# A fused two-layer matmul on one core: magnitude sums moved, a new start, and sums of w2 in another order

## The chip, the cores and the metric

The kernel runs on one core of one Trainium2 chip. The metric is the device time of one execution in microseconds (us). A run's time is its span in the profile plus about 1.55 us. All runs told here are of one core, and all were recorded as being in the fast one of the two states that a kernel's executions can show.

Engines are named as in the profile: PE multiplies, PEld loads its weights, DVE is VectorE, ACT is ScalarE, POOL is GpSimd, SP issues DMAs. A bank is the memory in which PE adds up products; in this kernel ACT or DVE reads it out before PE goes on in it.

## The reference

```python
y = np.matmul(x, w1) + b1      # x: 16 x 512 x 768 fp32, w1: 768 x 3072
y = np.maximum(y, 0)
return np.matmul(y, w2)        # w2: 3072 x 768, result fp32
```

## The kernel before

The rows of x (8192) are worked in blocks of 1024, and the 3072 hidden columns in two chunks. Each product is done by a Strassen-Winograd scheme: seven products in place of eight, with sums of the operands' quarters made by DVE. Block 0 multiplies x by w1 plainly (`first_plain`), since x and w1 come straight from the DMA then. ACT also makes magnitude sums of x, w1 and w2 (sums of squares, for w1 of fourth powers); only at the end are they looked at, to see whether fp16 was safe.

The parts that the change touches:

```python
def sums_w(self, w):                       # DVE, four sums of a weight tile
    for o, i, j in ((self.T3, self.B12, self.B22), (self.T1, self.B12, self.B11),
                    (self.T2, self.B22, self.T1), (self.T4, self.B21, self.T2)):
        self.nc.vector.tensor_tensor(out=w[:, o], in0=w[:, i], in1=w[:, j], op=ALU.subtract)
# T1 lies in the place of B12

def stat_w(self, stat, c, t, w):           # ACT, one magnitude sum
    ...
    if stat == "w1":
        self.nc.scalar.activation(out=junk, in_=src, func=ACTF.Square)
        src = junk
    self.nc.scalar.activation(out=junk, in_=src, func=ACTF.Square, accum_out=...)

# second(): one group of seven products of the second layer; bank "a" is used again and again
def p1(): mm(g["a"], self.A11, self.B11, True); copy("s1", g["a"], 0, 0)   # ACT copies
def p2(): ...                              # DVE adds to the output
def p6(): mm(g["a"], self.S2, self.T2, False); copy("s2", g["a"], 0, 1)    # needs p1's copy
...
def p7(): mm(g["a"], self.S3, self.T3, False); add(out(1, 1), g["a"], g["s5"])
def p4(): mm(g["a"], self.A22, self.T4, False); ...                        # needs p7's add

# run(): the start
self.transpose_x_first(0)                  # four row blocks of x, by PE, casts by DVE and ACT
self.turn_bias(rows)
# plan(): hooks that run after a named step, (group kind, block, group, step)
put("p1", 0, 1, 1, self.transpose_x_first, 1)      # the second 512 rows (xn), after t=1
...
```

The order of PE's work at the start is then: transposes of the first 512 rows, their products with w1 tiles 0 and 1, transposes of the second 512 rows (xn), their products with tiles 0 and 1, then tiles 2 to 5. A group's steps are interleaved with those of the next group, so between p1 and p6, and between p7 and p4, PE does three other steps.

## Time and profile before

| what | before |
|---|---|
| median of 4 runs | 907.83 us (906.83 to 907.95) |
| profiled run | 906.39 us, span 904.8 us |
| PE busy | 885.0 us, 98% of the span |
| PE's idle time that the waits name | 5.4 ACT, 5.2 first x, 1.4 sums of w2, 0.9 and 0.8 at the end |

The prediction shows the lines.

### The profile page before, as it was taken

What the parts mean: (1) busy time and instruction counts of PE and PEld (TensorE: products, weight loads), DVE (VectorE), ACT (ScalarE), POOL (GpSimd) and SP (SyncE); (2) the same over time, 40 slices, a digit from 0 to 9 for tenths busy, and PEclk for the clock granted to TensorE, in tenths of its full rate; (3) what the DMA queues carried; (4) which work ended last, traced back from release to release, by engine and by line L of the source; (5) the groups of instructions that cost most, each with busy time, mean ns of one, the idle gap of its engine ahead of it and who ended that gap; (6) DMA issues with size and microseconds to landing.
All of it is one profiled execution on the core that took longest, in us unless ns stands there. A gap on an engine that the chain in (4) does not pass through costs nothing. (4 is left out here: it accounts for less than half of the span.)

```text
span 904.8 us, 13016 instructions
## 1 busy us (share of the span) xinstructions
PE 885.0 (98%) x4775; PEld 468.7 (52%) x4775; DVE 551.9 (61%) x1013; ACT 425.0 (47%) x710; POOL 83.5 (9%) x143
## 2 busy tenths in 40 slices
PE   7999979999999999999999999999999999999997
PEld 4454444554545545455554545545455554545544
DVE  2597726557465565636737667576675757667564
ACT  4757696775555555534435048453513315042220
POOL 7200000000000100021101000100001010010100
PEclk9999999999999999999999999999999999999999
DMA  9999969678584964584849344644445354350613
GB/s 202 201 239 189 338 126 279 132 178 228 126 280 105 278 137 129 223 201 122 183 144 424 135 150 158 209 157 170 130 189 191 123 197 176 134 175 35 210 52 125
DMA packets 106471, 162.52 MB, mean 180 GB/s; under 512 B 67852, under 2 KB 81956, under 8 KB 104356
## 3 DMA queue, kind: packets, MB, share of 16 engines
q1 hardware_dynamic: 67696, 114.44, 36.6%
q0 software_dynamic: 38384, 46.41, 26.0%
q8 instruction: 39, 0.64, 0.3%
q10 hardware_dynamic: 324, 0.80, 0.2%
q14 instruction: 28, 0.23, 0.1%
HBM read 95.37 MB, written 76.48 MB: 190 GB/s over the span
## 5 line engine op out<-in xcount | busy, mean ns | idle before, releaser
L441 PEld LDWEIGHTS <-y 128*128 128x128 f16 x2688 | 263.4, 98 | 194.9 <-issue 10.2
L363 PEld LDWEIGHTS <-w1s 128*128 128x128 f16 x1890 | 185.0, 98 | 212.5 <-issue 1.7
L441 PE MATMUL a<-w2s,y 128*128 128x384 f16 x1536 | 277.5, 327 | 7.8 <-ACT s L454 5.4
L363 PE MATMUL a<-x,w1s 128*128 128x512 f16 x1080 | 267.8, 379 | 0.8 <-DVE y L373 0.8
L369 ACT ACTIVATE s<-a,b1y 128x512 f32<-128x512 f32 x180 | 123.7, 687 | 305.4 <-PE a L363 302.3
L363 PE MATMUL c<-x,w1s 128*128 128x512 f16 x540 | 145.9, 379 | 0.1
L441 PE MATMUL c<-w2s,y 128*128 128x384 f16 x768 | 145.7, 326 | 0.0
L319 DVE TENSOR_TENSOR y<-y 128x512 f16<-128x512 f16 x96 | 40.8, 425 | 116.1 <-ACT y L405 103.7
L446 DVE TENSOR_TENSOR o<-a,s 128x384 f32<-128x384 f32 x64 | 35.6, 556 | 83.4 <-PE a L441 73.3
L373 DVE CUSTOM_DVE_ANT_0 y<-a,s 128x512 f16<-128x512 f32 x90 | 61.7, 685 | 32.2 <-ACT s L369 32.0
L405 ACT ACTIVATE y<-a,b1y 128x512 f16<-128x512 f32 x90 | 61.8, 687 | 28.5 <-PE a L363 28.4
L441 PE MATMUL b<-w2s,y 128*128 128x384 f16 x384 | 73.2, 327 | 0.0
L363 PE MATMUL b<-x,w1s 128*128 128x512 f16 x270 | 73.0, 379 | 0.0
L426 POOL DMA_DIRECT2D o<-out_dram x64 | 34.1, 538 | 389.6 <-DMA out_dram<-o 225.6
L321 DVE TENSOR_TENSOR y<-y 128x1024 f16<-128x1024 f16 x96 | 66.4, 692 | 3.3
L369 ACT ACTIVATE s<-c,b1y 128x512 f32<-128x512 f32 x90 | 61.9, 688 | 8.1 <-PE c L363 8.1
L454 ACT ACTIVATE s<-a 128x384 f32<-128x384 f32 x64 | 31.3, 488 | 70.4 <-PE a L441 70.4
L373 DVE CUSTOM_DVE_ANT_0 y<-b,s 128x512 f16<-128x512 f32 x90 | 61.6, 684 | 3.0 <-PE b L363 1.3
L373 DVE CUSTOM_DVE_ANT_0 y<-c,s 128x512 f16<-128x512 f32 x90 | 61.5, 683 | 0.4
L446 DVE TENSOR_TENSOR o<-b,s 128x384 f32<-128x384 f32 x64 | 35.6, 556 | 26.3 <-PE b L441 15.6
L256 ACT ACTIVATE junk<-xn 128x768 f16<-128x768 f16 x60 | 50.5, 842 | 0.3
L446 DVE TENSOR_TENSOR s<-a,o 128x384 f32<-128x384 f32 x64 | 35.6, 556 | 19.5 <-PE a L441 19.5
(67 smaller groups left out, 421.7 us busy)
## 6 DMA issues: line engine op xcount, KB each, us to landing
out_dram<-o SPq DMA_DIRECT2D x127, 384.0 KB, 3.3
o<-out_dram POOLq DMA_DIRECT2D x64, 384.0 KB, 4.0
xd<-x SPq DMA_DIRECT2D x8, 2688.0 KB, 12.7
x<-xd SPq DMA_DIRECT2D x8, 2688.0 KB, 9.7
xn<-in_x_dram POOLq DMA_DIRECT2D x15, 768.0 KB, 10.6
w1s<-in_w_dram POOLq DMA_DIRECT2D x24, 192.0 KB, 6.6
w2d<-w2t SPq DMA_DIRECT2D x6, 672.0 KB, 4.4
w2s<-w2d SPq DMA_DIRECT2D x6, 672.0 KB, 9.3
```

What stands on the lines that cost most here:

```text
L256: self.nc.scalar.activation(out=junk[:, 0:2].rearrange("p a n -> p (a n)"), in_=rows, func=ACTF.Square, accum_out=self.stat[:, i:i + 1])
L319: tt(out=y[:, self.S1], in0=y[:, self.A21], in1=y[:, self.A22], op=ALU.add)
L321: tt(out=y[:, self.S3:self.S2 + 1:self.S2 - self.S3], in0=y[:, self.A21:self.S1 + 1], in1=a11, op=ALU.subtract)
L363: nc.tensor.matmul(ps, lhsT=w[:, slot, k, :], rhs=x[:, xslot, k, :], start=(start and k == 0), stop=(k == 2), skip_group_check=True)
L369: nc.scalar.activation(out=g[name], in_=ps, func=ACTF.Identity, bias=bias)
L373: nc.vector._custom_dve(TENSOR_ADD_SAT, out=y[:, slot], in0=ps, in1=g[s], s0=F_MAX, s1=0.0)
L405: nc.scalar.activation(out=y[:, self.A21], in_=g["a"], func=ACTF.Relu, bias=bias1)
L426: self.nc.gpsimd.dma_start(out=o[:, half, :], in_=self.rows_of(it, j, half))
L441: nc.tensor.matmul(ps, lhsT=ys[t][:, op, j * P:(j + 1) * P], rhs=ws[t][:, slot, :], start=(start and t == 0), stop=(t == self.TP - 1), ski ...
L446: nc.vector.tensor_tensor(out=o, in0=ps, in1=s, op=ALU.add)
L454: nc.scalar.activation(out=to, in_=ps, func=ACTF.Copy)
```

## The change

Three independent things. The magnitude sums of w1 and w2, which stood in blocks 1 and 2 two to a group, go one by one into the last groups of blocks 1 to 6 (those of the second chunk, in blocks 9 and 10 before, go one to a group into blocks 8 to 10). At the start PE works on a tile of ones until x comes, and the first rows are transposed and multiplied in two parts of 256 rows. And of the sums of w2, the two that are used first (T1, T2) are made first for all tiles, and T3, T4 after; T3 instead of T1 now lies in the place of B12. The sums of w1 use the same function, so they too are made in the new order, T1, T2, T3, T4.

```diff
+        every = ((self.T1, self.B12, self.B11), (self.T2, self.B22, self.T1),
+                 (self.T3, self.B12, self.B22), (self.T4, self.B21, self.T2))
...
-        self.transpose_x_first(0)
-        self.turn_bias(rows)
+        self.warm()                                  # nine products of ones
+        self.transpose_x_first(0, (0, 1))
+        self.hooks["p1", 0, 0, 0] = [lambda: self.transpose_x_first(0, (2, 3)),
+                                     lambda: self.turn_bias(rows)]
...
-            put("p1", 0, *at, lambda t: self.sums_w(self.w2s[t]), t)
+            put("p1", 0, *at, lambda t: self.sums_w(self.w2s[t], (0, 1)), t)
+        for t in range(TP):
+            put("p1", 0, 5, 3, lambda t: self.sums_w(self.w2s[t], (2, 3)), t)
...
-        for c in range(self.NCH):
-            for t in range(TP):
-                at = (t // 2, 1 + 3 * (t % 2))
-                put("m2", c * NSB + 1, *at, self.stat_w, "w1", c, t, self.w1s)
-                put("m2", c * NSB + 2, *at, self.stat_w, "w2", c, t, self.w2s)
+        for t in range(TP):
+            for n, (stat, ws) in enumerate((("w1", self.w1s), ("w2", self.w2s))):
+                put("m2", 1 + t, 3, 1 + 4 * n, self.stat_w, stat, 0, t, ws)
+                put("m2", NSB + t // 2, t % 2 * 2 + n, 3, self.stat_w, stat, 1, t, ws)
```

(Cut: `quarters`, which multiplies t=0 in two parts of 256 columns, and the memset of the ones, now on DVE.)

## The prediction

> **What bounds the kernel now.** I read the page first, then the waits of the matmul engine, then its timeline around each wait, then the other engines' timelines there. The page and the waits of PE (us in total, times, longest):
>
> ```profile
> PE 885.0 (98%) x4775; PEld 468.7 (52%) x4775; DVE 551.9 (61%) x1013; ACT 425.0 (47%) x710; POOL 83.5 (9%) x143
> PE a L441 <- ACT s L454: 5.4, 2, 4.2
> PE a L299 <- DMA o<-in_x_dram: 5.2, 1, 5.2
> PE a L441 <- DVE w2s L219: 1.4, 1, 1.4
> PE a L441 <- DVE s L446: 0.9, 1, 0.9
> ```
>
> PE is busy 885.0 of 904.8 us. So only about 20 us is idle, and the change removes few matmuls; it can win only those idle pieces and places where PE runs slowly. Three pieces belong to the three parts of the change: the start (5.2 us until x lands, then slow transposes), one wait for the sums of w2 (1.4 us, near 46 us), two waits for ScalarE (5.4 us, near 119 and 128 us). From 139.5 to 868.5 us PE is busy 728.79 of 728.97 us, so what is saved before stays saved.
>
> The timeline of the larger ScalarE wait (start, duration, in brackets idle before):
>
> ```profile
> 127.06 1.14 PE L441 MATMUL a<-w2s,y 128*128 128x384 f16 x6
> 132.41 2.08 PE L441 MATMUL a<-w2s,y 128*128 128x384 f16 x6 [4.21 <-ACT s L454]
> 134.28 1.51 PE L441 MATMUL b<-w2s,y 128*128 128x384 f16 x6
> 135.63 1.14 PE L441 MATMUL c<-w2s,y 128*128 128x384 f16 x6
> ...
> 126.32 1.48 ACT L231 ACTIVATE junk<-junk 128x1536 f16<-128x1536 f16 x1
> 127.71 0.19 ACT L231 ACTIVATION_READ_ACCUMULATOR junk<-junk 128x1 f32 x1
> 127.93 1.48 ACT L229 ACTIVATE junk<-w1s 128x1536 f16<-128x1536 f16 x1
> 129.44 1.48 ACT L231 ACTIVATE junk<-junk 128x1536 f16<-128x1536 f16 x1
> ```
>
> The reader sees two magnitude sums of w1 standing in ScalarE's queue ahead of the copy (L454) that PE needs. Six matmuls normally take 0.975 us from start to start; after the wait they take 1.87 and 1.35 us.
>
> The wait for w2, and DVE there:
>
> ```profile
> 44.95 0.98 PE L441 MATMUL a<-w2s,y 128*128 128x384 f16 x5
> 47.28 0.32 PE L441 MATMUL a<-w2s,y 128*128 128x384 f16 x1 [1.36 <-DVE w2s L219]
> ...
> 41.68 2.98 DVE L219 TENSOR_TENSOR w2s<-w2s 128x384 f16<-128x384 f16 x8
> 44.58 0.42 DVE L319 TENSOR_TENSOR y<-y 128x512 f16<-128x512 f16 x1
> 46.10 1.53 DVE L219 TENSOR_TENSOR w2s<-w2s 128x384 f16<-128x384 f16 x4
> 47.54 0.55 DVE L446 TENSOR_TENSOR o<-b,s 128x384 f32<-128x384 f32 x1
> ```
>
> DVE has no gap from 34.3 to 51 us and 11.5 of 14 us are busy from 56 to 70: work pushed to later here collides with a full engine.
>
> **What the skill says.** The Trainium skill, "TensorE: Matmul & The Clock Gate", Part 1, says that PE starts at half clock until some 3.4 us of activity and falls back after an idle window of about that length. The trace agrees: the fp32 transposes of x keep a spacing of 0.64 us for three until about 8.4 us and 0.33 us after, and the 4.21 us wait is followed by matmuls at half speed. Its Part 4 says that transposes do not bring the full clock on; here they are the only PE work before the clock doubles, so the trace disagrees. "Perfetto Trace Analysis", Tensor Engine Instruction, says that ACT and DVE queues are strictly first in, first out; the copy behind two sums, above, agrees. "DMA: Bandwidth & Descriptors", Issuing engines are not separate DMA queues, says that all issuers share the same 16 engines. The DMA view agrees: by 7 us the queue that POOL feeds (q0: w1, then the second 512 rows of x) has moved 0.06 MB, while the first rows took 1.6 MB; by 9 us 0.42, by 15.3 us 1.67 MB.
>
> **Part 1, the sums spread over blocks.** Before, in block 1 six w1 sums (1.48 + 1.48 + 0.19 = 3.15 us each) stand two to a group of seven products (6.8 us), beside copies of 4 x 0.49 and, in two of the groups, squares of x of 4 x 1.03 us: 6.3 + 2.0 + 4.1 = 12.4 us of work in 6.8. After, each of blocks 1 to 6 has one w1 and one w2 sum (3.15 + 1.67 us), both in its last group, where no square stands: 4.8 + 2.0 = 6.8 us at most in 6.8, and half of that group is interleaved with the next product's, where ScalarE's timeline shows gaps of 2.4 and 2.6 us per step. The copy of a group is needed three steps later (2.9 us), and block 2, with two w2 sums per group beside squares, lost only 0.09 us. So both waits go: 1.20 + 4.21 = 5.41 us. The slow matmuls after go too: (1.87 - 0.975) + (1.35 - 0.975) = 1.27 us. Sum: **6.7 us gained**. In the second chunk of w1, ScalarE is half idle, and the sums there were free and stay so.
>
> **Part 2, the start.** Nine products of ones warm the clock, then two of four row blocks are transposed, then w1 tile 0 is multiplied in quarters. But what releases the work that follows? Block t=1 is followed in order by the transposes of the second half of x (xn). In the trace these begin at 15.27 us, right when PE was free:
>
> ```profile
> 10.04 1.46 PE L335 MATMUL a<-x,w1s 128*128 128x512 f16 x6 [0.15 <-DVE x L305]
> 13.92 1.46 PE L335 MATMUL c<-x,w1s 128*128 128x512 f16 x6
> 15.27 1.41 PEld L299 LDWEIGHTS <-xn 128*128 128x128 f16 x24 [0.38 <-DMA xn<-in_x_dram]
> ```
>
> xn was issued at 6.43 and needs 8.8 us to landing: 15.23 us. It hardly moves (POOL loses one memset of 0.14 us), so no gain of the start can pass this point: at most 0.1 or 0.2 us. And w1 tile 0 bounds the quarters: its halves were issued at 1.50 and about 2.4 us and land 6.7 and about 6.9 us later, at 8.2 and 9.3 us. Step by step at full clock: four groups of transposes 5.2 to 6.5, casts ready at about 7.0; quarter products with the first half 8.2 to 8.9 (6 x 0.109), wait, with the second half 9.3 to 9.9; twelve transposes 9.9 to 11.2; DVE's cast (0.2 + 0.56 us after its transposes) until 11.65; twelve products of 256 columns to 13.0; t=1 twelve of 0.216 to 15.6 us. Transposes of xn then start at 15.6 instead of 15.27: **0.3 us lost**. The old order had the fp32 transposes inside the time in which w1 was on its way; the new one puts half of them after it.
>
> **Part 3, the sums of w2 in order of use.** Before, PE waits for the third of four sums of tile 5 (T2), ready at 47.2. After, only T1 and T2 of each tile come early; DVE is free when ACT's last ReLU ends (43.89), makes the sums of y 43.9 to 45.4 and T1, T2 of tile 5 to 46.2: PE resumes at 46.25 instead of 47.28, **1.03 us gained**. But T3 and T4 of all six tiles, 12 x 0.37 us, now stand right behind, to 50.6. PE's product that needs T3 would run 48.4 to 49.35 and must have T3 of tile 5, the eleventh: 46.2 + 11 x 0.37 = 50.25, so it ends at 50.5 (1.15 lost). DVE then is 3.1 us behind (first add at 50.6 against 47.54), with these in order: add 0.47, sums of x 0.98 + 1.68, and only at 53.75 the add that frees bank a for the fourth product: ready at 54.36, due at 53.41 (0.95 lost). The same for the next group: 1.45 + 0.47 + 0.86 + 2.9 + 0.87 us of DVE work before its add, ready 61.85, due 61.18 (0.67 lost). Then the sum of x for the next block, ready 67.33, due 67.04 (0.29). After that DVE has caught up, as it had 2.1 us idle before 69.18. Sum 3.06 lost, 1.03 gained: **2.0 us lost**.
>
> Total: 907.7 - 6.7 + 0.3 + 2.0 = **903.3 us**.
>
> **Rivals.** (1) The order of w2 pays as meant: PE can take T3 of tile 0 early, and DVE's backlog is hidden; then that part gains up to 1.4 us and the time is about 900. Against it speaks DVE's strict order and its full row from 40 to 66 us. (2) The start gains what it saves in front of the first product (2 us) because xn or w1 land earlier: 899 to 901. Against: both DMA times follow from bytes behind the first rows of x, which do not change. (3) The start loses more: the clock is not up in time, since PE waits in between, and the quarter products or transposes run at half speed, 1 to 2 us more: 905. For it: gaps of 1 to 2 us remain before 9.3 us. (4) The new sums in the last groups of six blocks make a small wait each (0.3 us x 6): 905; against it the gaps above.
>
> **Range and chances.** Part 1 is the surest, 6 to 7 us. Start: -0.2 to +1.5. w2: -1 to +3. Together 901.0 to 905.5. A change of 2% would be 18 us, out of reach of a kernel with 20 us of idle: faster 0.01, same 0.98, slower 0.01.
>
> **What would show it.** Right: no wait of PE for ACT L454 near 119 to 133; transposes of xn starting at 15.2 to 15.8, whatever the first product's start; a wait for DVE's w2 sums of about 0.4 us near 46 and of about 1 us near 50, then waits for DVE's adds near 54 and 61. Wrong: first xn transposes before 15 us, PE without wait between 46 and 68, or waits for ACT in the last groups of blocks 1 to 6.

## The result

The changed kernel takes 899.61 us (median of 4 runs, 899.57 to 899.70), against 907.83 us. The ratio is 0.9912 (95% interval 0.9895 to 0.9929). Ratios here are the mean time of one kernel's fast runs over that of the other's of the same rounds, so not quite the ratio of the medians. The gain is 8.2 us; 4.4 were predicted, and 899.61 lies below the range. The class, within 2%, was right.

PE's waits in the profile after (us in total, times, longest):

```profile
PE b L239 <- DVE ones L156: 1.3, 1, 1.3
...
PE a L361 <- DMA w1s<-in_w_dram: 0.7, 1, 0.7
PE a L468 <- DVE o L473: 0.6, 1, 0.6
PE a L468 <- DVE w2s L220: 0.3, 1, 0.3
```

(Cut: the two waits at the end, 0.9 and 0.8 us as before.) The waits for ACT are gone, the wait for the sums of w2 has shrunk from 1.4 to 0.3 us, and two new ones stand there: for w1 tile 0 at the start, and for DVE's add to `o`.

The timeline of the changed kernel where the long wait was:

```profile
126.06 2.11 PE L468 MATMUL a<-w2s,y 128*128 128x384 f16 x12
...
131.91 1.14 PE L468 MATMUL c<-w2s,y 128*128 128x384 f16 x6
132.88 0.81 PE L390 MATMUL a<-x,w1s 128*128 128x512 f16 x3
```

PE has no gap there (the lines left out follow each other at 0.975 us for six matmuls); the product of the next block's first layer begins at 132.88 us, where before it began at 139.53.

The timelines of both kernels at three landmarks give a balance. Products for w2 begin at 43.00 before and at 43.59 after: the start lost 0.59 us. A step after both w2 waits (p5 of the second group) stands at 54.27 and at 54.63: lost 0.36 by then, so the sums of w2 gained 0.23. The landmark just named is 6.65 us earlier, so the spread sums gained 7.01. The rest of the span is 765.3 and 765.1 us (these four figures are differences of the landmarks and spans). That makes 6.8 us between the two profiles (904.8 to 898.0), and 8.2 between the medians. The other 1.4 us is a question for the experiments: it belongs to runs of before that were not profiled.

The start after:

```profile
1.29 4.21 PE L239 MATMUL b<-ones 128*128 128x128 f32 x18 [1.29 <-DVE ones L156]
5.40 0.87 PE L307 MATMUL a<-ident,o 128*128 128x128 f32 x3
...
7.15 0.49 PE L307 MATMUL c<-ident,o 128*128 128x128 f32 x3
8.38 0.83 PE L361 MATMUL a<-x,w1s 128*128 128x256 f16 x6 [0.74 <-DMA w1s<-in_w_dram]
9.45 0.83 PE L361 MATMUL c<-x,w1s 128*128 128x256 f16 x6 [0.24 <-DMA w1s<-in_w_dram]
...
15.81 0.33 PE L307 MATMUL a<-ident,xn 128*128 128x128 f16 x3
```

The first product comes 1.7 us earlier than before (8.38 against 10.04), yet the transposes of xn come 0.54 us later (15.81 against 15.27).

DVE's sums of w2 after, from queries of single moments (start, duration): a run of 14 sums, and the starts of its first three.

```profile
46.04 3.97 DVE L220 TENSOR_TENSOR w2s<-w2s 128x384 f16<-128x384 f16 x14
...
46.04 0.35 DVE L220 TENSOR_TENSOR w2s<-w2s 128x384 f16<-128x384 f16 x1
46.43 0.36 DVE L220 TENSOR_TENSOR w2s<-w2s 128x384 f16<-128x384 f16 x1
46.70 0.35 DVE L220 TENSOR_TENSOR w2s<-w2s 128x384 f16<-128x384 f16 x1
```

And before, the four sums of the last tile, T3, T1, T2, T4:

```profile
46.10 0.35 DVE L219 TENSOR_TENSOR w2s<-w2s 128x384 f16<-128x384 f16 x1
46.48 0.36 DVE L219 TENSOR_TENSOR w2s<-w2s 128x384 f16<-128x384 f16 x1
46.87 0.36 DVE L219 TENSOR_TENSOR w2s<-w2s 128x384 f16<-128x384 f16 x1
47.27 0.36 DVE L219 TENSOR_TENSOR w2s<-w2s 128x384 f16<-128x384 f16 x1
```

In the old order every sum starts 0.38 to 0.40 us after the one before it. In the new one T2 starts 0.39 us after T1, which it reads, but the next, T3, starts 0.27 us after T2, and the fourteen should take 0.39 + 12 x 0.27 + 0.35 = 3.98 us; 3.97 were measured.

### The profile page after: what moved, and what is told of

It reads as the page before. It is cut to its first block, busy times and chain, and to the rows that moved or that the text cites. A ratio compares the mean times of both kernels' runs of the same rounds, so it can differ in the third digit from the quotient of the medians.

```text
span 898.0 us, 13078 instructions
## 1 busy us (share of the span) xinstructions
PE 887.0 (99%) x4805; PEld 472.2 (53%) x4805; DVE 548.5 (61%) x1014; ACT 425.5 (47%) x710; POOL 83.6 (9%) x142
```

## The experiments

Twelve kernels in three calls; all gave correct results. "Old" and "new" are the ways of before and after. The kernel before was timed in every call, at medians of 907.83, 907.75, 907.76 and 908.02 us; so where a kernel is set against the 899.61 of the changed one, up to some 0.3 us can come from the call. no_start, w2_old, w2_unsplit and fill_gap share one call.

### before_again: the kernel before, unchanged

> The kernel before, unchanged, to see how its executions differ. Its four timed runs span 906.83 to 907.95 us and its profiled one took 906.39, while the changed kernel's lie within 0.13 us. Theory C (clock): the length of the half-speed stretch after the 4.2 us wait for ScalarE differs from run to run; so the spans of the runs differ by 1 us or more, the longer ones have the lower mean clock, and in the new profile the matmuls after the wait are slow for another time than the 1.27 us lost in the first profile. Rival R: the spread comes from the start, where the clock rises at a time that differs; then the new profile differs from the first before 43 us and not after 119.

Measured: 907.44 us (907.00 to 907.73, 5 runs), ratio to before 0.9998. What theory C expected of the runs did not come: they span 0.73 us and not 1, and the longer ones do not have the lower mean clock (0.997 at 907.00 and 907.73, 0.998 at 907.59). Of the 0.6 us between the two profiled runs the start holds most, as rival R has it: by the spacing of single transposes (0.213 us, then 0.109) the clock doubles at about 9.4 us and not at 8.7, and the products for w2 begin at 43.48, not 43.00. The stretch after the long wait holds a little: it costs 0.895 + 0.495 us (1.87 and 1.47 for 0.975) and not 1.27. Of the seven profiles with the old start, the first one is the quickest: in the others the products for w2 begin at 43.22 to 44.12 us.

### stats_only: only the magnitude sums new

> Only the magnitude sums are spread over blocks; start and w2 sums as before. From the two traces this part is worth 1.36 + 4.38 us of waiting and 1.27 us of half-speed matmuls, 7.0 us, and 0.1 us near 190. Theory C: span 904.8 - 7.1 = 897.7, so 899.3 us in all, with all runs within 0.3 us, that is a little faster than the whole change. Rival R: median near 900.7 and a spread of about 1 us, as the start is the old one. My prediction's number for it alone was 901.1.

The diff is the last hunk of the change, applied to the kernel before. Measured: 899.23 us (899.08 to 900.10, 4 runs), ratio 0.9906. The whole gain is here, and more: 8.5 us by the medians. Three runs lie at 899.1 to 899.3; the profiled one, at 900.10, has a start in which all eight groups of transposes ran at half clock (the last at 9.94 us), and the products for w2 began at 43.89. So the rival's mechanism exists: this start is 0.9 us later than the first profile's, and the runs of this kernel, which has no long wait, spread over 1.0 us.

### old_stats: start and sums of w2 new, magnitude sums old

> The changed kernel with the magnitude sums put back where they were, so new start and new order of w2 sums only. By the traces the start costs 0.6 us and the order of w2 gains 0.2 us: 907.8 + 0.4 = 908.2 us. Theory C: runs spread by about 1 us as those of before. Rival R: within 0.3 us, near 906.8. The prediction had these two parts at +2.3 us: 910.1.

```diff
 the last hunk of the change is taken back
```

Measured: 907.44 us (906.63 to 908.24, 4 runs), ratio 1.0000 (0.9985 to 1.0016). New start and new order together change nothing that can be seen; 908.2 was expected. The runs spread over 1.6 us though the start is the new one, as theory C has it. The two longest have the lowest mean clocks, 0.996 (907.83 us) and 0.994 (908.24 us), but the shortest has 0.997 (906.63) and the next 0.998 (907.05), so the order is not strict. In the profiled run, the shortest, the long wait is again followed by slow matmuls, which cost 1.37 us:

```profile
132.68 2.08 PE L468 MATMUL a<-w2s,y 128*128 128x384 f16 x6 [4.21 <-ACT s L481]
134.56 1.60 PE L468 MATMUL b<-w2s,y 128*128 128x384 f16 x6
136.00 1.14 PE L468 MATMUL c<-w2s,y 128*128 128x384 f16 x6
```

Against the changed kernel, whose runs lie within 0.13 us, the old magnitude sums thus cost from 7.0 us (906.63) to 8.6 us (908.24).

### one_moved: one of the two sums ahead of the long wait moved

```diff
-                put("m2", c * NSB + 1, *at, self.stat_w, "w1", c, t, self.w1s)
+                put("m2", c * NSB + 1, *((3, 1) if (c, t) == (0, 3) else at), self.stat_w, ...)
```

> The kernel before, but one of the two w1 sums in front of the long wait (tile 3, 3.15 us on ScalarE) moved to the last group of the same block. The wait of 4.4 us should shrink to about 1.2 us. If waits cost only their length, the gain is 3.2 us: 904.6. If, as theory C says, a wait of 4.4 us also brings half-speed matmuls that last 1.3 us in the profiled and about 2.7 us in the usual run, and one of 1.2 us does not, the gain is 4.4 to 5.9 us: about 902.0 with the runs within 0.3 us.

Measured: 907.94 us (907.55 to 909.55, 5 runs), ratio 1.0004. It missed, as an experiment on the length of the wait. The wait at 128 us shrank to 1.25 us from start to start as meant, but the moved sum came to stand right behind that of tile 5, and the two held up a copy a group later. The profile still tells something:

```profile
140.25 2.08 PE L441 MATMUL a<-w2s,y 128*128 128x384 f16 x6 [3.58 <-ACT s L454]
142.12 1.48 PE L363 MATMUL b<-x,w1s 128*128 128x512 f16 x3
143.40 2.12 PE L441 MATMUL c<-w2s,y 128*128 128x384 f16 x6
145.32 1.26 PE L363 MATMUL a<-x,w1s 128*128 128x512 f16 x3
146.42 1.14 PE L441 MATMUL a<-w2s,y 128*128 128x384 f16 x6
```

Here the slow stretch lasts from 140.25 to 146.42 us, 6.2 us, for work that takes 2 x (0.975 + 0.65) = 3.25 us at full clock: 2.9 us lost after a wait, against 1.27 in the first profile.

### one_moved2: the same sum moved further away

```diff
+                put("m2", *((2, 3, 1) if (c, t) == (0, 3) else (c * NSB + 1, *at)), self.stat_w, ...)
```

> One_moved did not do what it was meant to: the moved sum came to stand behind that of tile 5 and the long wait only moved. Now the sum of tile 3 goes to the last group of block 2, far from the others. The waits of 1.36 and 4.38 us become 1.36 and about 1.25, and none after. If a wait costs only its length: 907.75 - 3.1 = 904.6 us, spread as before. If a wait of 4.4 us also brings half speed for a time that differs (1.3 to 3 us lost in the traces so far) and one of 1.25 us does not: 901.7 to 903.3, and the runs lie closer together than those of before, apart from the start's own spread (up to 0.9 us).

Measured: 904.80 us (904.56 to 905.49, 5 runs), before in the same rounds 908.02 us; ratio 0.9964. The number is that of "only its length", but the trace does not bear that out. The moved sum, now behind w2's, caused a wait of 1.74 us in block 2, and one of 0.46 us was uncovered in block 1. All ACT waits come to 4.5 us, against 5.4 before, and from start to start to 5.2 against 5.7. So PE waits only about 0.6 us less, yet from the first product for w2 to the end this profile is 2.0 us shorter than the first one (859.8 against 861.8). No wait is longer than 1.74 us, and the matmuls after it are not slow (1.14 us for six, where the slow ones have 2.08):

```profile
193.94 1.14 PE L441 MATMUL a<-w2s,y 128*128 128x384 f16 x6 [1.74 <-ACT s L454]
```

The other 1.4 us is close to the 1.27 that the slow stretch cost in the first profile. By the medians it would be 2.6 us (3.2 less 0.6), but that holds the starts as well: this profile, the longest of the five runs, has the latest start of all (44.12 us). That one wait of 4.4 us costs more than its length is thus shown; how much more in a usual run is not.

### no_start: the changed kernel with the old start

```diff
-        self.warm()
-        self.transpose_x_first(0, (0, 1))
+        self.transpose_x_first(0)
+        self.turn_bias(rows)
 (and no quarters, no hook after t=0, the memset of the ones on POOL)
```

> The changed kernel with the old start (no products of ones, all of the first rows transposed before the first product, memset on POOL). By the traces the new start begins the products for w2 at 43.5 to 43.6 us, the old one at 43.0 to 43.9 us depending on when the clock rises. Theory: the new start gains nothing in usual runs, as both must wait for the second half of x, and costs up to 0.6 us: 899.0 us with an odd run near 900. Rival (warming pays): 900.0 or more.

Measured: 899.25 us (899.12 to 899.99, 4 runs), so three runs 0.3 to 0.5 us faster than the changed kernel and one 0.4 slower. The new start does not pay in time. It makes the time steadier: with the new sums, each of the three kernels that have the old start shows one of four runs 0.7 to 0.9 us above its others (stats_only, no_start, best), and no kernel with products of ones spreads over more than 0.4 us.

### warm_only: products of ones, but no quarters

```diff
         self.warm()
-        self.transpose_x_first(0, (0, 1))
+        self.transpose_x_first(0)
+        self.turn_bias(rows)
 (and no quarters, no hook after t=0)
```

> The changed kernel with the products of ones, but then all sixteen... all four row blocks transposed and t=0 whole, in the old order; no quarters. If the landing of the second half of x is what binds the start, PE must wait for it here (about 2 us, first transposes of xn near 15.4 us), the products for w2 start near 43.2, and the time is 899.2 to 899.3 in every run, with no odd run near 900 as in no_start. If instead the earlier first product were worth something, under 898.5.

Measured: 899.13 us (898.95 to 899.35, 4 runs): no odd run near 900, and 0.5 us faster than with quarters.

```profile
13.41 1.46 PE L343 MATMUL c<-x,w1s 128*128 128x512 f16 x6
15.28 0.34 PE L307 MATMUL a<-ident,xn 128*128 128x128 f16 x3 [0.42 <-DMA xn<-in_x_dram]
```

The first products began at 9.53 us and were over by 14.9, and PE waited for xn until 15.28, for 0.4 us and not the 2 us that I expected. In best_warm below the first products began at 9.11, and after a wait of 0.9 us the transposes of xn at 15.38. So the landing of xn is the limit of the start, as the prediction said; the quarters cost what they put behind it.

### w2_old: the changed kernel with the old sums of w2

```diff
-            put("p1", 0, *at, lambda t: self.sums_w(self.w2s[t], (0, 1)), t)
-        for t in range(TP):
-            put("p1", 0, 5, 3, lambda t: self.sums_w(self.w2s[t], (2, 3)), t)
+            put("p1", 0, *at, lambda t: self.sums_w(self.w2s[t]), t)
 (and the old order T3, T1, T2, T4, with T1 in B12's place)
```

> The changed kernel with the sums of w2 (and w1) in the old order and place. By the traces of before and after the new order gains 1.03 us at the first wait and gives back 0.04 and 0.78 at two later ones: net 0.2 us, so 899.8 us. My prediction had the new order lose 2.0 us: then this kernel would be at 897.6. A rival in which the order pays in full (1.4 us) would give 901.0.

Measured: 899.76 us (899.70 to 899.87, 4 runs), 0.15 us slower than the changed kernel; the two traces give 0.2. The order of w2 is a small gain and not the loss of 2.0 us that I predicted.

### w2_unsplit: new order within a tile, nothing deferred

```diff
-            put("p1", 0, *at, lambda t: self.sums_w(self.w2s[t], (0, 1)), t)
-        for t in range(TP):
-            put("p1", 0, 5, 3, lambda t: self.sums_w(self.w2s[t], (2, 3)), t)
+            put("p1", 0, *at, lambda t: self.sums_w(self.w2s[t]), t)
```

> The changed kernel with the new order inside a tile (T1, T2, T3, T4) but all four sums of a tile together at the old places, nothing deferred. Theory D: a sum that needs the one just before it starts 0.385 us after it, one that does not starts 0.27 us after; the old order is a chain of three such steps per tile, the new one has one. Then four sums take 1.28 us (from the first start to the last end) and not 1.53, DVE is ahead by itself, T2 of the last tile comes when it does in the changed kernel, T3 right behind, and the add that frees bank a is in time: no wait of PE for o, 0.8 us less than the changed kernel: 898.8. If deferring is what gains (the intent of the change), this is slower than 899.6.

Measured: 898.80 us (898.75 to 898.87, 4 runs), as expected, and 0.96 us less than w2_old in the same rounds. The timeline of DVE:

```profile
45.98 1.28 DVE L220 TENSOR_TENSOR w2s<-w2s 128x384 f16<-128x384 f16 x4
47.17 0.55 DVE L473 TENSOR_TENSOR o<-b,s 128x384 f32<-128x384 f32 x1
```

Four sums take 1.28 us and not 1.53, and the first add follows at 47.17 (49.92 in the changed kernel). The only wait left in this stretch is the 0.3 us for T2. What gains is the order inside a tile; deferring T3 and T4 gives most of it back.

### fill_gap: late sums put into DVE's idle time

```diff
+            at = (5, 2) if t == 5 else at
             put("p1", 0, *at, lambda t: self.sums_w(self.w2s[t], (0, 1)), t)
         for t in range(TP):
-            put("p1", 0, 5, 3, lambda t: self.sums_w(self.w2s[t], (2, 3)), t)
+            at = (5, 2) if t < 3 else (5, 3)
+            put("p1", 0, *at, lambda t: self.sums_w(self.w2s[t], (2, 3)), t)
```

> The changed kernel with T1, T2 of the last tile and T3, T4 of the first three tiles put into the 2.2 us in which DVE waits for the last ReLU (42.3 to 44.5 us), and only T3, T4 of three tiles after. Expected: no wait of PE for w2s (0.45 us) nor for o (0.78 us): 899.6 - 1.25 = 898.3. If these waits are covered by others, less.

Measured: 898.32 us (898.18 to 898.45, 4 runs). PE has no wait for w2 or for `o` at all.

### best and best_warm: faster than both kernels

> Spread sums, the gap filled as in fill_gap, and the old start: fill_gap 898.3 less what no_start gained (0.36 us): 897.9, with an odd run 0.8 us later.

> Spread sums, the gap filled as in fill_gap, products of ones but no quarters: 898.3 less what warm_only gains over the changed kernel (0.3 to 0.4 us): 897.9 in every run.

Both are fill_gap with another start: the old one (best), or ones without quarters (best_warm). Measured: 898.09 us (897.91 to 898.92) and **897.72 us** (897.64 to 897.93), 4 runs each; ratio of the latter to before 0.9887 (0.9872 to 0.9902). It is 1.9 us faster than the changed kernel by the medians (1.8 by the profiled spans), and steady. Both gaps to what was expected are under 0.2 us.

The profiles of all runs can be compared without their starts, from the first product for w2 to the end of the span (us, a difference of the two):

| kernel | w2 products begin | from there to the end |
|---|---|---|
| before, before_again | 43.00, 43.48 | 861.8, 862.0 |
| old_stats | 43.50 | 861.6 |
| one_moved, one_moved2 | 43.72, 44.12 | 864.3, 859.8 |
| stats_only, w2_old | 43.89, 43.51 | 854.6, 854.6 |
| changed kernel | 43.59 | 854.4 |
| no_start, warm_only | 43.37, 42.98 | 854.3, 854.4 |
| w2_unsplit | 43.52 | 853.7 |
| fill_gap, best, best_warm | 43.50, 43.22, 43.07 | 853.1, 853.1, 853.1 |

Seen so, the magnitude sums are worth 7.2 us. Against the old sums of w2 (w2_old) the changed kernel gains 0.2, the new order inside a tile alone 0.9, and the filled gap 1.5.

## Why the prediction was wrong

**The bound and the places** were right: PE's idle time near 5, 46 and 128 us, and nothing after 140 us.

**Part 1** was right in mechanism (ahead of the copy stood also a square of x, 0.84 + 0.19 us, which its lines leave out): both ACT waits and the slow matmuls went, and no group of blocks 1 to 6 got a new wait. The sum was too small, 6.7 us. Two terms were mis-sized. The waits were read as 1.20 + 4.21, but the profile counts idle time from the modelled end of the last matmul; from start to start they cost 1.36 + 4.38, together 0.33 more. And the 1.27 us of slow matmuls was taken from the one profiled run. Among the kernels with a wait of about 4 us, the traces show 1.27, 1.39, 1.37 (old_stats) and 2.9 us, and with the start held steady the time of old_stats moves by 1.6 us. By the medians the part is worth 8.5 us (stats_only), by the traces 7.2; the 1.3 us between the two are not explained by any trace. Of the 1.4 us that the two first profiles leave unexplained, some 0.5 is probably the lucky start of before's (43.00, where the seven profiles of the old start have a median of 43.48). That the rest is a longer slow stretch in the runs without a trace is argued and not shown. For it speaks that old_stats spreads over 1.6 us and the changed kernel, with the same start, over 0.13; the mean clocks bear it out only in part (old_stats, but not before_again).

**Part 2** was right in its limit (landing of xn, shown by warm_only) and in its sign. I expected the transposes of xn at 15.6; they came at 15.81. Two readings were off, and only one of them counted. The clock was not up when x came (it doubled at about 6.9 us), as rival 3 feared, but after these transposes PE waited 0.74 us for w1 all the same. In old_stats, with the same start, the clock doubled 1.1 us sooner, the wait for w1 was 1.17 us, and the transposes of xn came at 15.72, only 0.09 sooner. Most of the delay is that the second half of w1 tile 0 held PE until 9.45, not 9.3. The 0.59 us between the two profiles is an overstatement, as the first profile had a lucky start; no_start puts the cost at 0.36 us by the medians.

**Part 3** contains the step that failed: "T3 and T4 of all six tiles, 12 x 0.37 us". The 0.37 was the mean spacing of the old sums, which are chains. In the new order most sums neither read what the one just before wrote nor write where it read, and they start every 0.27 us. So the twelve sums took 3.2 us (46.70 to 49.92) where 4.4 were charged. The first half of the part was exact: PE was to resume 1.03 us earlier, and did (46.84 with a start 0.59 later, against 47.28). But DVE's first add came at 49.92, not at 50.6 + 0.59, and of the four losses of 1.15, 0.95, 0.67 and 0.29 us, the traces show 0.04, 0.78 (of which the profile counts 0.6 as idle), none and none:

```profile
51.90 1.14 PE L468 MATMUL a<-w2s,y 128*128 128x384 f16 x6
53.66 1.14 PE L468 MATMUL a<-w2s,y 128*128 128x384 f16 x6 [0.61 <-DVE o L473]
...
49.92 0.55 DVE L473 TENSOR_TENSOR o<-b,s 128x384 f32<-128x384 f32 x1
...
53.05 0.55 DVE L473 TENSOR_TENSOR o<-a,s 128x384 f32<-128x384 f32 x1
```

The later sums of w1 ran faster too, 1.28 us for four in place of the 1.45 that I charged from start to next start (now 1.20). So the part gained 0.15 to 0.23 us instead of losing 2.0. Of the miss of 3.7 us this is 2.2; most of the rest lies in part 1. Rival 1 (the order pays) was thus right in sign, and partly in its reason: the backlog was mostly hidden, but because DVE's work shrank, which neither side had in view.

Why a dependent sum starts 0.12 us later can be read further in the packed traces, which keep each instruction's semaphores (the counters by which instructions wait for each other). In five of them (before, changed, w2_old, w2_unsplit, fill_gap) there are 290 pairs of sums of w1 or w2 that follow each other without a pause. In 162 the two start 0.38 us or more apart; there the second waits for a semaphore of DVE itself and starts 0.034 to 0.035 us after the end of the first. That is just the number of pairs in which the second depends on the first, three in a tile of the old order and one in a tile of the new. In the 128 others the two start 0.27 to 0.28 us apart, and the second starts 0.08 us or more before the end of the first; 43 of these wait for DVE's semaphore too, but for an earlier sum. So the 0.12 us is the wait for the end of the neighbour. No run took this wait out and left all else as it was.

## What to carry to other kernels

A spacing read from a row of instructions belongs to their order: before a move, ask whether the neighbours depend on each other, because the same instructions may run closer afterwards. One profile is one run: where PE waited about 4 us here, the half-speed stretch after it cost 1.27 to 2.9 us in four traces, so the gain of removing the wait is larger and less certain than its length. And an earlier first product is worth nothing if the next thing PE needs lands when it did.

## What the Trainium skill lacked or had wrong

- "TensorE: Matmul & The Clock Gate", Part 4, says that transposes do not bring the full clock on. In five of the seven profiles with the old start the clock doubled while fp32 transposes were PE's only work: their spacing (three) went from 0.64 to 0.33 us, 3.5 us after the first of them in before, 4.0 in before_again. In the other two (stats_only, one_moved2) all eight groups ran at half clock, and it doubled at about the first product. The profile shows these transposes as matmuls with the identity; whether they use the transpose mode that the page speaks of is not in it.
- The same page, Part 1, puts the warm-up at about 3.4 us, with some 0.5 us either way from run to run. From PE's first work to the double clock it took 3.4 to 5.9 us here in the seven profiles with the old start and 4.1 to 6.1 in the seven with products of ones. After a wait the slow stretch here lasted about 3 us in the first profile (132.41 to 135.63 us) and 6.2 us in one_moved; that it can take nearly twice the page's figure is not there. That a wait of 1.74 us keeps the full clock and one of 3.58 us does not (one_moved2, one_moved) agrees with it.
- "VectorE: DVE Perf Modes", The DRAIN you can't avoid, says that the next operation does not start until the pipe is empty, that one which is not held starts earlier, and, from a chain of copies, that a semaphore costs nothing extra. Here sums of 128x384 fp16, 0.35 us long, start every 0.27 us when independent, inside the one before, which fits the second statement. They start every 0.385 us when a sum waits for the semaphore of the one just before; that differs from the third. No page gives a spacing for such a waiting sum, and the difference was the largest term of the miss.
- No page says that the clock row of a profile can miss the start, though the clock page, Part 1, warns that clock events in a trace have been unreliable: the windows view of before has a granted clock of 1.00 from 5.19 to 15.27 us, while the fp32 transposes ran at half their later pace until about 8.7.
